# Group A's keys by residue of 16, strided attention on runs of 8 keys, and its queries copied by GpSimd

## The chip, the core and the metric

The program runs on one core of one Trainium2 chip. A core has TensorE (matmuls from SBUF into PSUM), VectorE, ScalarE, GpSimd, and SyncE, which issues the transfers; 16 DMA engines move data between HBM and SBUF. The engines run in parallel, each takes its own instructions in order, and they wait for each other through semaphores. The metric is the time of one execution on the device in microseconds.

## What is computed

One layer of a decoder with four groups of four heads (A to D), sequence 2048, head dimension 64. After a projection, each group attends in its own way, and the gated results go through an output projection. The change is in group A, which attends three times and merges: over 129 neighbours (rate 1), over every 4th token, and over every 16th.

```python
DILATED_CONFIGS = ((128, 1), (512, 4), (2048, 16))

def dilated_attention(q, k, v, table_h):
    b, nh, s, dh = q.shape
    outs, lses = [], []
    for window, rate in DILATED_CONFIGS:
        fold = lambda t: t.reshape(b, nh, s // rate, rate, dh).transpose(0, 3, 1, 2, 4).reshape(b * rate, nh, s // rate, dh)
        o, lse = banded_attention(fold(q), fold(k), fold(v), table_h, window // rate, dist_scale=rate)
...
    wts = jax.nn.softmax(jnp.stack(lses, axis=0), axis=0)
    return jnp.sum(wts[..., None] * jnp.stack(outs, axis=0), axis=0).astype(q.dtype)

def banded_attention(q, k, v, table_h, max_dist, dist_scale=1, sink=None):
    # query m attends keys m-j, 0 <= j <= max_dist, in blocks of 128 queries
...
    s = jnp.einsum('bhnqd,bhnkd->bhnqk', qb, kk).astype(jnp.float32) * (dh ** -0.5)
...
    s = s + rel_bias(dist * dist_scale, table_h).transpose(2, 0, 1)[:, None]
    p, m, den = masked_probs(s, valid, sink)
    o = jnp.einsum('bhnqk,bhnkd->bhnqd', p, vv.astype(jnp.float32)) / den

def reference(x, ...):
    h = rms_norm(x, norm_w[layer]) @ w_in[layer]
...
    o_a = dilated_attention(rms_norm(heads(a_q), g[0]), rms_norm(heads(a_k), g[1]), heads(a_v), tables[0])
...
    y = jnp.concatenate([merge(o_a), merge(o_b), merge(o_c), merge(o_d)], axis=-1) * jax.nn.silu(silu_gate)
    x = x + y @ w_out[layer]
```

## The kernel before

The kernel projects the groups in the order C, D, A, B, and attends in the order C, D, then A and B together. Projections and the output projection are written as generators of small steps, "fillers". A driver (`drive`) keeps a modelled clock for every engine (`T`), advanced by `op` with an expected duration for each instruction, and picks the next step for TensorE: attention steps whose inputs the model says are there, otherwise a filler step. The resulting order is fixed when the program is built; on the chip only semaphores decide when each instruction runs.

For queries and keys, `project` normalises a tile of 128 tokens and `turn` (L741) transposes it, four tiles at a time, from 128 tokens x 128 features into PSUM as features x tokens. `split` writes a high and a low half (two numbers that add up to the value) to HBM, `tqA` and `tkA`, tokens in order.

Strided attention of group A (`make_a`, `a_unit`) runs over 4 heads, rates 16 and 4, and 4 values of q0: 32 units. A unit has four blocks j of 128 queries. `qk_load` brings the whole head's queries (`wb` or `AQ`) and keys (`wb` or `keys`) into SBUF, tokens in order, for even and odd heads in turn; the next head's loads are issued in six pieces during units 1 to 6 of the current head. A score (L1639) is two matmuls per block: the block's 128 queries are the weights, 128 or 256 keys are the moving columns. Both are slices with a step of r words. At rate 16 a block has 128 keys; at rate 4 all blocks but the first of a residue have 256 (own and previous block): per head and rate 32 matmuls, at rate 4 24 of them with 256 columns.

Behind a half unit's scores VectorE adds the bias and takes the maximum (L1644, one reduction per block), scales the two maxima by -1 (L1649), ScalarE exponentiates (L1655), TensorE transposes the weights (L393), ScalarE and VectorE split them (L399, L403), TensorE multiplies with the values (L422), ScalarE copies the result (L371), TensorE transposes it back (L435) and VectorE adds its two halves (L439). After rate 4 of each head the two rates are merged, on GpSimd in the main (L1754, L1756), and stored.

Then 16 units of rate 1 of group A (`make_a1`) alternate with 16 units of group B (`make_b`, scores in L1941). The rate-1 units use the same `a_unit` with keys in contiguous slices, 60 of their 64 blocks with 256 keys.

The output projection (`out_proj`) is the filler of this part of the program: a tile's y and gate are loaded, gated (GpSimd L2102), transposed (L2112), and multiplied with the output weights (L2148) in 64 runs of 12 matmuls of 512 columns in all, first for groups C and D, then for A and B.

The planner's cost of a score and the two slices stand in these lines:

```python
e = op("PE", mm(n) if r == 1 else max(217.0, 0.92 * n)) + 60.0
...
c0 = rho + r * 128 * (i - i0)
return slice(c0, c0 + (n - 1) * r + 1, r)
```

Of the kernel before, what the change touches and what calls it, by code (L numbers as in the profile page):

```python
# [102 lines left out]
def tile_hybrid_heads(ctx, tc, a):  # L103
# [527 lines left out]
    def project(g, first=None):  # L631
# [104 lines left out]
        def turn(t3, j, gi, keep):  # L736
# [3 lines left out]
            for i in range(4):  # L740
                PE.transpose(ps[:, i * 128:(i + 1) * 128], keep[i][0][:, j * 128:(j + 1) * 128], ident)  # L741
# [827 lines left out]

    def qk_load(h, x):  # L1570

        q, k = QK[h % 2]
        n = S // 2
        if x < 2:
            aready[h] = load_q(q[:, x * n:(x + 1) * n].unsqueeze(1), "A", h, 1, x * n, n)
        else:
            c = slice((x - 2) // 2 * n, ((x - 2) // 2 + 1) * n)
            aready[h] = mv(raw(k)[x % 2::2, :, c], TK["A"][h * 64:h * 64 + 64, :, c])

# [29 lines left out]
    def group_ab():  # L1609
      with tc.tile_pool(name="aw", bufs=2) as aw, tc.tile_pool(name="as", bufs=1) as as_:  # L1610
# [8 lines left out]


        def a_unit(r, q0, setup, room, need, source, stats, close):
# [5 lines left out]
            def scores(half):  # L1627
# [7 lines left out]
                for j in (2 * half, 2 * half + 1):  # L1635
                    n = 128 * (1 + prevs[j])
                    s0 = (j % 2) * 256
                    for x in range(2):
                        PE.matmul(ps[:, s0:s0 + n], lhsT=qs(j), rhs=ks(x, j, prevs[j]), start=(x == 0), stop=(x == 1))  # L1639
                        e = op("PE", mm(n) if r == 1 else max(217.0, 0.92 * n)) + 60.0  # L1640
                for j in (2 * half, 2 * half + 1):
                    n = 128 * (1 + prevs[j])
                    s0 = (j % 2) * 256
                    V.tensor_tensor_reduce(P[:, j, :n], ps[:, s0:s0 + n], rev(H, n - 1, n), 1.0, LOW,  # L1644
                                           OP.add, OP.max, mx[:, j:j + 1])
                    e = op("DVE", vv(n), e)
# [11 lines left out]
                defer(e, weights)  # L1658

# [22 lines left out]
        def make_a(n):  # L1682
# [8 lines left out]

            def setup():
                if h < 3 and 1 <= n % 8 <= 6:
                    qk_load(h + 1, n % 8 - 1)
                if q0 == 0:
# [80 lines left out]
            def room():  # L1776
                if not have_all("A"):
# [3 lines left out]
            u = a_unit(r, q0, setup, room, lambda: max(at("s"), aready[h]), source,  # L1781
                       lambda: tiles(res[h, r][0]), close)
# [39 lines left out]
        def make_a1(m):  # L1822
            q0, h = AORDER[m]

            def source():
                Q, K, lo = As[m][0], As[m][1], As[m][7]
                return ((lambda j: Q[:, j * 128:(j + 1) * 128]),
                        (lambda x, j, p: K[:, x, (q0 + j - p - lo) * 128:(q0 + j + 1 - lo) * 128]), raw(A1H(h)))
# [12 lines left out]
            def setup():  # L1841
                if m == 0:
# [3 lines left out]
                    parts += [as_.tile([128, 1024], F32R, name="ow%d" % i) for i in range(2)]  # L1846
# [180 lines left out]
    def out_weights(half, places):  # L2027


        def load(i, after=0.0):  # L2030
            k, c = OCH[i]
            rw = px.tile([128, 512], F32, name="raw", bufs=4)
            r0 = ROW0[half] + k * 128
            e = mv(rw, a["w_out"][r0:r0 + 128, c * 512:(c + 1) * 512], after)
            if half == "CD" and i in olocked:
                oparked[i] = (e, lambda: split(i, rw, e))
            else:
                defer(e, lambda: split(i, rw, e))

        def split(i, rw, e):  # L2040
# [5 lines left out]
            def low():  # L2046
                V.scalar_tensor_tensor(l, rw, 0.5, h, op0=OP.mult, op1=OP.subtract)
                oready[half, OCH[i]] = op("DVE", vv(512) + 62.0, e)
                if i + OAHEAD < 8:
# [6 lines left out]
    def out_proj():  # L2056
# [19 lines left out]
        def load(n):  # L2076
# [3 lines left out]
            for i, g in enumerate(half):  # L2080
                mv(yt[:, i * 256:(i + 1) * 256], y_d[g][rows, :])
            gt = px.tile([128, 512], F32, name="raw", bufs=4)
            e = mv(gt, gate_d[rows, ROW0[half]:ROW0[half] + 512])
            defer(e, lambda: gate(n, yt, gt, e))
# [8 lines left out]
        def gate(n, yt, gt, e):  # L2093
# [5 lines left out]
            def rest():  # L2099
                V.scalar_tensor_tensor(th, th, 1.0, gt, op0=OP.add, op1=OP.mult)  # L2100
                e2 = op("DVE", vv(512), e)
                G.tensor_tensor(yt, yt, th, op=OP.mult)  # L2102
# [124 lines left out]
```

## Time and profile before

| | |
|---|---|
| time, median of 3 runs | 1796.22 us (1788.68 to 1797.0) |
| profiled execution | 1786.75 us, of which the span of instructions is 1785.0 |
[...]
| TensorE matmuls | busy 96% of the span |
| VectorE, ScalarE, GpSimd | busy 75%, 60%, 39% |
| HBM | 172 GB/s over the span |

Busy shares are means over stages that have different limits; the last 425 us, from 1360 us on, hold everything that the change touches but the key transposes. Matmuls overlap, so a matmul's duration isn't what the next one waits; the distance from one start to the next is. Line numbers are those of the kernel before.

### The profile page before, as it was taken

What the parts mean: (1) busy time and instruction counts of PE and PEld (TensorE: products, weight loads), DVE (VectorE), ACT (ScalarE), POOL (GpSimd) and SP (SyncE); (2) the same over time, 40 slices, a digit from 0 to 9 for tenths busy, and PEclk for the clock granted to TensorE, in tenths of its full rate; (3) what the DMA queues carried; (4) which work ended last, traced back from release to release, by engine and by line L of the source; (5) the groups of instructions that cost most, each with busy time, mean ns of one, the idle gap of its engine ahead of it and who ended that gap; (6) DMA issues with size and microseconds to landing.
All of it is one profiled execution on the core that took longest, in us unless ns stands there. A gap on an engine that the chain in (4) does not pass through costs nothing.

```text
span 1785.0 us, 31766 instructions
## 1 busy us (share of the span) xinstructions
PE 1715.9 (96%) x10035; PEld 1503.3 (84%) x10035; DVE 1332.7 (75%) x4072; ACT 1072.1 (60%) x2586; POOL 688.4 (39%) x841
## 2 busy tenths in 40 slices
PE   7989999999998999899989999999999999999999
PEld 5878878888787888688877889999879998888887
DVE  5446778998899996688567778887167777888883
ACT  4445556666676765567555667676256776576661
POOL 4666564544454554112353632222521111423231
PEclk9999999999999999999998999999999999999999
DMA  7763554344446324831485333323375768999986
GB/s 244 227 206 115 165 170 159 99 125 138 125 130 202 100 93 144 229 102 57 142 250 180 123 93 86 109 62 96 103 239 163 233 209 266 293 326 304 303 280 215
DMA packets 283480, 308.24 MB, mean 173 GB/s; under 512 B 80256, under 2 KB 201216, under 8 KB 282640
## 3 DMA queue, kind: packets, MB, share of 16 engines
q1 hardware_dynamic: 283312, 306.21, 55.7%
q8 instruction: 80, 1.31, 0.3%
q14 instruction: 88, 0.72, 0.1%
HBM read 219.47 MB, written 86.92 MB: 172 GB/s over the span
## 4 chain that ended last, share of the span: by engine, by line
PE 44%; DMA 4%; DVE 4%; issue 3%; POOL 2%; SPq 1%; ACT 1%; POOLq 0%; DVEq 0%; ACTq 0%
PE o L422 8%; PE j L833 8%; PE j L2148 7%; PE pt L393 7%; PE s L943 4%; PE s L1639 3%; PE pt L435 2%; PE s L1329 1%; DMA wb<-tkA 1%; SPq L156 1%; DMA DQ<-tqD 1%; PE s L1428 1%; PE pt L2112 1%; POOL xl L577 1%; PE s L1941 0%
## 5 line engine op out<-in xcount | busy, mean ns | idle before, releaser
L833 PE MATMUL j<-wb,xh 128*128 128x512 f32 (+2 forms) x2048 | 619.4, 383 | 12.6 <-ACT wb L618 8.0
L833 PEld LDWEIGHTS j<-wb,xh 128*128 128x128 f32 x2048 | 372.4, 191 | 58.6 <-issue 12.2
L833 PE MATMUL j<-wb,xl 128*128 128x512 f32 (+2 forms) x1024 | 386.1, 377 | 1.3 <-POOL xl L577 1.3
L403 DVE TENSOR_TENSOR pl<-pt,ph 128x512 fp32r<-128x512 f32 (+4 forms) x486 | 312.0, 659 | 40.6 <-ACT ph L399 40.2
L399 ACT ACTIVATE ph<-pt 128x512 fp32r<-128x512 f32 (+4 forms) x486 | 265.3, 575 | 123.5 <-PE pt L393 116.8
L833 PEld LDWEIGHTS j<-wb,xl 128*128 128x128 f32 x1024 | 194.7, 190 | 27.7 <-POOL xl L577 2.7
L679 POOL TENSOR_TENSOR ss<-ss,expo 128x6 f32<-128x6 f32 (+2 forms) x64 | 117.1, 1829 | 213.6 <-DVE ss L677 202.3
L577 POOL TENSOR_TENSOR xl<-xt,xh 128x512 fp32r<-128x512 f32 x112 | 150.1, 1340 | 9.3
L371 ACT ACTIVATE ot<-o 128x512 f32<-128x512 f32 (+1 forms) x160 | 81.5, 509 | 108.9 <-PE o L422 108.4
L943 PE MATMUL s<-keys,Q 128*128 128x512 f32 (+3 forms) x320 | 113.1, 400 | 10.9 <-DVE mx L945 5.5
L2102 POOL TENSOR_TENSOR xt<-xt,sq 128x512 f32<-128x512 f32 x32 | 41.3, 1289 | 197.9 <-DVE sq L2100 85.8
L571 POOL TENSOR_SCALAR xh<-xt 128x512 fp32r<-128x512 f32 x128 | 85.5, 668 | 76.4 <-DMA xt<-in_xt_dram 47.5
L660 ACT ACTIVATE stqk<-j 128x512 f32<-128x512 f32 x64 | 38.3, 598 | 122.5 <-PE j L833 122.3
L945 DVE CUSTOM_DVE_ANT_0 prow<-s,Hs 128x512 f32<-128x512 f32 (+3 forms) x160 | 94.6, 606 | 18.1 <-PE s L943 11.4
L674 DVE TENSOR_REDUCE ss<-sq 128x6 f32<-128x384 f32 (+2 forms) x64 | 39.4, 616 | 92.0 <-ACT sq L664 91.9
L1059 DVE SCALAR_TENSOR_TENSOR pa<-pb,ra,pa 128x1024 f32<-128x1024 f32 (+4 forms) x96 | 103.5, 1105 | 2.3
L945 DVE CUSTOM_DVE_ANT_0 pa<-s,H 128x512 f32<-128x512 f32 (+3 forms) x160 | 93.7, 604 | 14.4 <-PE s L943 12.6
L1655 ACT ACTIVATE ap<-ap,AO 128x128 f32<-128x128 f32 (+1 forms) x192 | 86.4, 454 | 18.6 <-DVE AO L1649 16.7
L945 DVE CUSTOM_DVE_ANT_0 pb<-s,H 128x512 f32<-128x512 f32 (+3 forms) x160 | 92.8, 604 | 4.3 <-PE s L943 3.5
L435 PE MATMUL pt<-ident,ot 128*128 128x128 f32 x512 | 85.4, 279 | 5.2 <-ACT ot L371 5.0
L1043 ACT ACTIVATE pa<-pa,nm 128x128 f32<-128x128 f32 (+7 forms) x64 | 76.9, 1201 | 21.6 <-DVE nm L951 21.1
L1523 ACT ACTIVATE prow<-prow,nm 128x128 f32<-128x128 f32 (+7 forms) x64 | 76.8, 1201 | 15.3 <-DVE nm L951 7.3
(266 smaller groups left out, 4201.7 us busy)
## 6 DMA issues: line engine op xcount, KB each, us to landing
xt<-in_xt_dram SPq DMA_DIRECT2D x128, 256.0 KB, 3.5
xr<-in_x_dram SPq DMA_DIRECT2D x16, 512.0 KB, 5.6
Q<-tqC SPq DMA_DIRECT2D x64, 128.0 KB, 3.4
DQ<-tqD SPq DMA_DIRECT2D x16, 512.0 KB, 4.5
raw<-gate_d SPq DMA_DIRECT2D x32, 256.0 KB, 4.3
stqk<-in_x_dram SPq DMA_DIRECT2D x32, 256.0 KB, 4.8
acc_d<-stqk SPq DMA_DIRECT2D x32, 256.0 KB, 4.5
stqk<-acc_d SPq DMA_DIRECT2D x32, 256.0 KB, 4.1
```

What stands on the lines that cost most here:

```text
L393: PE.transpose(ps[:rows, x * 128:(x + 1) * 128], src(), ident)
L399: A.activation(ph[:rows, :n], ps[:rows, :n], AF.Copy)
L403: V.tensor_tensor(pl[:rows, :n], ps[:rows, :n], ph[:rows, :n], op=OP.subtract)
L422: PE.matmul(u["po"][:, c0:c0 + wd], lhsT=lhsT(), rhs=x[:rows, col:col + wd], start=u["k"] == 1, stop=u["k"] == total, skip_group_check=True)
L435: PE.transpose(ps[:, i * 128:(i + 1) * 128], ot[:, i * 128:(i + 1) * 128], ident)
L577: G.tensor_tensor(l, xt, h, op=OP.subtract)
L679: G.tensor_tensor(ss[:, :nh], ss[:, :nh], expo[:, :nh], op=OP.pow)
L833: PE.matmul(ps[:, :n], lhsT=xx[:, ks], rhs=W[k][ww][:, lo:hi], start=(k == 0 and i == 0), stop=(k == KT - 1 and i == 2))
L943: PE.matmul(ps[:, :n], lhsT=q(), rhs=k[:, k0:k0 + n], start=(i == 0), stop=(i == np_ - 1))
L945: V.tensor_tensor_reduce(st["row"][:, k0:k0 + n], ps[:, :n], rev(H, t * 128 + 127 - k0, n), 1.0, LOW, OP.add, OP.max, st["mx"][:, ci:ci + 1])
L1059: V.scalar_tensor_tensor(rows[i][:, k0:k0 + n], part[i][:, k0:k0 + n], ra[:, 1:2], rows[i][:, k0:k0 + n], op0=OP.mult, op1=OP.add)
L2148: PE.matmul(ps, lhsT=xx[:, ks], rhs=OW[half, (k, c)][ww], start=(x == 0 and k == 0 and i == 0), stop=(x == len(halves) - 1 and k == 3 and ...
```

## The change

Keys of group A are stored in another order. Inside each tile of 128 tokens, token 16 i + r goes to place 8 r + i: all tokens of one residue of 16 lie side by side, in runs of 8. The reordering is done by the key transposes (`turn`, j >= 2), which write their PSUM columns with a step.

- Rate 16 reads 16 runs of 8 keys, one of each tile, in the right order.
- Rate 4 reads four runs of 8 from each tile (a residue of 4 holds four residues of 16); its score columns come out as (residue, run), and VectorE's reduction reads them from PSUM with a step to put them back in order.
- Rate 1 reads its one or two tiles residue by residue, in runs of 8, and its reduction reads with a step likewise.

The strided queries are no longer weights with a step: `gather_more` has GpSimd copy the four blocks of a unit side by side into one of four slots of 512 columns (two tiles `ow0`, `ow1`, which before were taken later for output weights). A slot is free when the unit that read it has its scores; the copies for the next head wait until its load is expected. The planner counts 1150 ns for a copy and, for a strided score, the same as for a contiguous one. Besides, the buffers `raw` of the output projection are now tracked by the planner, which holds back a load while none is free.

```diff
@@ turn
-                PE.transpose(ps[:, i * 128:(i + 1) * 128], keep[i][0][:, j * 128:(j + 1) * 128], ident)
+                to = ps[:, i * 128:(i + 1) * 128]
+                if g == "A" and j >= 2:
+                    to = to.rearrange("p (r i) -> p i r", r=16)
+                PE.transpose(to, keep[i][0][:, j * 128:(j + 1) * 128], ident)
@@ group_ab
+        OW4 = [as_.tile([128, 1024], F32R, name="ow%d" % i) for i in range(2)]
+        AC = {}
+
+        def gather_more():
+            while len(AC) < len(ORDER) and ORDER[len(AC)][0] in aloaded and free("AC", 4) < INF:
+                n = len(AC)
+                h, r, q0 = ORDER[n]
+                hd = alloc("AC", 4)
+                C = OW4[hd[1] % 4 // 2][:, hd[1] % 2 * 512:hd[1] % 2 * 512 + 512]
+                Q = QK[h % 2][0].rearrange("p (c r) -> p r c", r=r)
+                if r == 16:
+                    G.tensor_copy(C.rearrange("p (j c) -> p j c", j=4), Q[:, q0:q0 + 4])
+                else:
+                    G.tensor_copy(C, Q[:, q0 // 4])
+                AC[n] = (C, hd, op("POOL", 1150.0, max(aready[h], hd[2])))
@@ a_unit, scores
-                        e = op("PE", mm(n) if r == 1 else max(217.0, 0.92 * n)) + 60.0
+                        e = op("PE", mm(n)) + 60.0
...
-                    V.tensor_tensor_reduce(P[:, j, :n], ps[:, s0:s0 + n], rev(H, n - 1, n), 1.0, LOW,
+
+                    fr = ps[:, s0:s0 + n] if r == 16 else ps[:, s0:s0 + n].rearrange("p (b u) -> p u b", b=16 // r)
+                    V.tensor_tensor_reduce(P[:, j, :n], fr, rev(H, n - 1, n), 1.0, LOW,
@@ make_a
+            def scored():
+                release(AC[n][1], T["PE"] + 60.0)
+                defer(T["PE"] + 100.0, gather_more)
...
-                Q, K = QK[h % 2]
-
-                def cols(j, i0, n):
-                    rho, i = divmod(q0 + j, nb)
-                    c0 = rho + r * 128 * (i - i0)
-                    return slice(c0, c0 + (n - 1) * r + 1, r)
-                return (lambda j: Q[:, cols(j, 0, 128)]), (lambda x, j, p: K[:, x, cols(j, p, 128 * (1 + p))]), Hs[h, r]
+                K, C = QK[h % 2][1], AC[n][0]
+                if r == 16:
+                    K = K.rearrange("p x (t r c) -> p x r t c", t=16, r=16)
+                    ks = lambda x, j, p: K[:, x, q0 + j]
+                else:
+                    K = K.rearrange("p x (t s a c) -> p x a s t c", s=4, a=4, c=8)[:, :, q0 // 4]
+                    ks = lambda x, j, p: K[:, x, :, (j - p) * 4:(j + 1) * 4]
+                return (lambda j: C[:, j * 128:(j + 1) * 128]), ks, Hs[h, r]
@@ make_a1, source
-                        (lambda x, j, p: K[:, x, (q0 + j - p - lo) * 128:(q0 + j + 1 - lo) * 128]), raw(A1H(h)))
+                        (lambda x, j, p: K[:, x].rearrange("p (t b c) -> p b t c", b=16, c=8)[:, :, q0 + j - p - lo:q0 + j + 1 - lo]),
+                        raw(A1H(h)))
@@ out_proj, prepare
-            while n < min(len(PARTS), at_["part"] + 3) and (n < 2 or n - 2 in zready) and there(*PARTS[n]):
+            while n < min(len(PARTS), at_["part"] + 3) and (n < 2 or n - 2 in zready) and there(*PARTS[n]) and free("raw", 4) < INF:
```

The new costs also move instructions. On TensorE, at the first units of strided attention (head 0, rate 16), `s` is a score, `j` the output projection, `pt` a transpose of gated rows (`xt`) or of attention weights (`ap`). Before:

```order
L1639 MATMUL s<-wb 128x128 x12
L2148 MATMUL j<-wb,xh 128x512 x2
L2148 MATMUL j<-wb,xl 128x512
L1639 MATMUL s<-wb 128x128 x4
L2112 MATMUL pt<-ident,xt 128x128 x4
L393 MATMUL pt<-ident,ap 128x128 x4
L1639 MATMUL s<-wb 128x128 x12
L393 MATMUL pt<-ident,ap 128x128 x4
```

Of the change:

```order
L1663 MATMUL s<-wb,ow_17186 128x128 x8
L2190 MATMUL j<-wb,xh 128x512 x2
L2190 MATMUL j<-wb,xl 128x512
L1663 MATMUL s<-wb,ow_17186 128x128 x8
L2190 MATMUL j<-wb,xh 128x512 x2
L2190 MATMUL j<-wb,xl 128x512
L393 MATMUL pt<-ident,ap 128x128 x4
L1663 MATMUL s<-wb,ow_17187 128x128 x8
L2190 MATMUL j<-wb,xh 128x512 x2
L2190 MATMUL j<-wb,xl 128x512
L2154 MATMUL pt<-ident,xt 128x128 x4
```

Where one step of the output projection stood among the first 28 scores, three stand now. Counted over the whole order, 75 matmuls of the output projection stood between the first strided score and the first rate-1 score, and 153 do now; between the first score of the first rate-1 unit and that of the last 420 and now 393; behind that 231 and now 177.

On GpSimd, around the merge of head 0 (`AO`), with copies of queries (`ow`) and gating (`xt`) beside it. Before:

```order
L2102 TENSOR_TENSOR xt<-xt,sq 128x512 x3
L1754 TENSOR_TENSOR AO<-AO,mg 128x16x65 x2
L1756 TENSOR_TENSOR AO<-AO 128x16x65
L1757 COPY AO<-mgn 128x16
```

Of the change:

```order
L1638 COPY ow_17186<-AQ 128x512 x2
L1638 COPY ow_17187<-AQ 128x512 x2
L1640 COPY ow_17186<-AQ 128x512
L2144 TENSOR_TENSOR xt<-xt,sq 128x512
L1640 COPY ow_17186<-AQ 128x512
L1640 COPY ow_17187<-AQ 128x512 x2
L1791 TENSOR_TENSOR AO<-AO,mg 128x16x65 x2
L1793 TENSOR_TENSOR AO<-AO 128x16x65
L1794 COPY AO<-mgn 128x16
```

The eight copies of head 1 stand ahead of the first merge, one gating among them; the copies stand in the same queue as gating and merges.

## Rows read from the trace of the kernel before

**Rows 1.** The page, part 1 (busy time, share, instructions) and part 4 (chain).

```profile
PE 1715.9 (96%) x10035; PEld 1503.3 (84%) x10035; DVE 1332.7 (75%) x4072; ACT 1072.1 (60%) x2586; POOL 688.4 (39%) x841
...
PE 44%; DMA 4%; DVE 4%; issue 3%; POOL 2%; SPq 1%; ACT 1%; POOLq 0%; DVEq 0%; ACTq 0%
```

**Rows 2.** Busy us of each engine in three stretches, granted clock, DMA share, GB/s.

```profile
1363.00:1500.00 137.00, 135.87 (x848) 129.88 (x846) 100.94 (x407) 98.34 (x342) 24.35 (x16) 1.00 0.76 241
1501.00:1727.00 226.00, 220.18 (x1452) 194.96 (x1450) 193.78 (x659) 152.68 (x459) 71.52 (x97) 1.00 0.95 295
1735.00:1785.00 50.00, 46.22 (x213) 37.46 (x211) 20.32 (x32) 6.56 (x12) 9.78 (x10) 0.99 0.69 222
```

**Rows 3.** Groups by line and shape, 1360 to 1500: busy us, mean ns, idle before.

```profile
L1639 PEld LDWEIGHTS s<-keys,AQ 128*128 128x128 f32 x128 | 30.8, 318 | 0.4 <-DVE amx L1644 0.3
...
L422 PEld LDWEIGHTS o<-ph,tl 128*128 128x128 f32 x59 | 11.4, 193 | 0.0
```

**Rows 4.** TensorE's timeline, strided scores of head 0: start, length, instruction, count.

```profile
1367.85 2.83 PE L1639 MATMUL s<-wb 128*128 128x128 f32 x12
1370.49 0.62 PE L393 MATMUL pt<-ident,ap 128*128 128x128 f32 x4
1370.87 1.09 PE L1639 MATMUL s<-wb 128*128 128x128 f32 x4
...
1380.12 2.23 PE L1639 MATMUL s<-wb 128*128 128x256 f32 x8
1382.16 0.24 PE L422 MATMUL o<-ph,th 128*128 128x128 f32 x1
```

**Rows 5.** TensorE's timeline, contiguous operands: products of head 0, rate-1 scores.

```profile
1372.10 0.27 PE L422 MATMUL o<-pl,tl 128*128 128x128 f32 x1
1372.21 0.27 PE L422 MATMUL o<-ph,tl 128*128 128x128 f32 x1
...
1609.20 1.20 PE L1639 MATMUL s<-wb 128*128 128x256 f32 x8
1610.24 0.63 PE L2148 MATMUL j<-wb,xh 128*128 128x512 f32 x2
```

**Rows 6.** VectorE's groups by line and shape, whole span: reductions, scaling, PSUM reads.

```profile
L403 DVE TENSOR_TENSOR pl<-pt,ph 128x512 fp32r<-128x512 f32 x388 | 259.4, 684 | 33.0 <-ACT ph L399 32.7
L1649 DVE TENSOR_SCALAR AO<-amx 128x2 f32<-128x2 f32 x96 | 24.6, 256 | 3.6
L1644 DVE CUSTOM_DVE_ANT_0 ap<-s,wb 128x256 f32<-128x256 f32 x60 | 23.1, 419 | 3.9 <-PE s L1639 3.9
L1644 DVE CUSTOM_DVE_ANT_0 ap<-s,AH 128x256 f32<-128x256 f32 x48 | 18.9, 419 | 4.4 <-PE s L1639 4.4
L439 DVE TENSOR_REDUCE AO<-pt 128x256 f32<-128x512 f32 x27 | 18.6, 689 | 18.0 <-PE pt L435 18.0
L775 DVE TENSOR_TENSOR sq<-pt,post 128x512 f32<-128x512 f32 x8 | 8.8, 1104 | 0.7 <-PE pt L741 0.7
```

**Rows 7.** GpSimd's groups by line and shape, whole span: 512-word operations.

```profile
L577 POOL TENSOR_TENSOR xl<-xt,xh 128x512 fp32r<-128x512 f32 x112 | 150.1, 1340 | 9.3
L571 POOL TENSOR_SCALAR xh<-xt 128x512 fp32r<-128x512 f32 x128 | 85.5, 668 | 76.4 <-DMA xt<-in_xt_dram 47.5 <-PE j L833 16.6 <-PE o L422 5.7
```

**Rows 8.** All engines' timeline around a merge on GpSimd at 1443.9.

```profile
1443.21 0.42 DVE L1644 CUSTOM_DVE_ANT_0 ap<-s,AH 128x256 f32<-128x256 f32 x1 [0.54 <-PE s L1639]
...
1443.91 3.82 POOL L1754 TENSOR_TENSOR AO<-AO,mg 128x1040 f32<-128x1040 f32 x2 [29.39 <-ACT mg L1751]
1444.02 1.85 DVE L1649 TENSOR_SCALAR AO<-amx 128x2 f32<-128x2 f32 x1
```

**Rows 9.** TensorE's timeline in the tail: output projection alone.

```profile
1735.48 0.62 PE L2148 MATMUL j<-keys,xh 128*128 128x512 f32 x2
1735.94 0.40 PE L2148 MATMUL j<-keys,xl 128*128 128x512 f32 x1
1736.17 0.62 PE L2148 MATMUL j<-keys,xh 128*128 128x512 f32 x2
```

More of the change, by code (lines that the diff above doesn't have):

```diff
@@ L1568, in tile_hybrid_heads @@
     aready = {}
+    aloaded = set()
     def qk_load(h, x):
@@ L1578, in qk_load @@
             aready[h] = mv(raw(k)[x % 2::2, :, c], TK["A"][h * 64:h * 64 + 64, :, c])
+        if x == 5:
+            aloaded.add(h)
     ORDER = [(h, r, q0) for h in range(4) for r in (16, 4) for q0 in range(0, 16, 4)]
@@ L1617, in h_load, with a_unit @@
             Hs[h, r] = H
-        def a_unit(r, q0, setup, room, need, source, stats, close):
+        OW4 = [as_.tile([128, 1024], F32R, name="ow%d" % i) for i in range(2)]
[12 more added lines that the diff above has]
+                AC[n] = (C, hd, op("POOL", 1150.0, max(aready[h], hd[2])))
+        def a_unit(r, q0, setup, room, need, source, stats, close, scored=lambda: None):
             nb = 16 // r
@@ L1658, in scores @@
                 defer(e, weights)
+                if half:
+                    scored()
             jobs = []
@@ L1690, in tiles @@
                 return O[:, q0:q0 + 4] if nb == 1 else O[:, q0 // nb::r]
+            def scored():
+                release(AC[n][1], T["PE"] + 60.0)
+                defer(T["PE"] + 100.0, gather_more)
             def setup():
+                if n == 0:
+                    gather_more()
                 if h < 3 and 1 <= n % 8 <= 6:
                     qk_load(h + 1, n % 8 - 1)
+                    if n % 8 == 6:
+                        defer(aready[h + 1], gather_more)
                 if q0 == 0:
@@ L1779, in room @@
                 return 0.0 if q0 else free("AO", 4)
-            u = a_unit(r, q0, setup, room, lambda: max(at("s"), aready[h]), source,
-                       lambda: tiles(res[h, r][0]), close)
+            u = a_unit(r, q0, setup, room, lambda: max(at("s"), aready[h], AC[n][2] if n in AC else INF), source,
+                       lambda: tiles(res[h, r][0]), close, scored)
             u["after"] = after
@@ L1845, in setup @@
                     parts += [QK[1][0][:, i * 1024:(i + 1) * 1024] for i in range(2)]
-                    parts += [as_.tile([128, 1024], F32R, name="ow%d" % i) for i in range(2)]
+                    parts += OW4
                     out_weights("AB", [(w[:, 0:512], w[:, 512:1024]) for w in parts])
@@ L2031, in load, with split @@
             k, c = OCH[i]
+            hd = alloc("raw", 4)
             rw = px.tile([128, 512], F32, name="raw", bufs=4)
             r0 = ROW0[half] + k * 128
-            e = mv(rw, a["w_out"][r0:r0 + 128, c * 512:(c + 1) * 512], after)
+            e = mv(rw, a["w_out"][r0:r0 + 128, c * 512:(c + 1) * 512], max(after, hd[2]))
             if half == "CD" and i in olocked:
-                oparked[i] = (e, lambda: split(i, rw, e))
+                oparked[i] = (e, lambda: split(i, rw, e, hd))
             else:
-                defer(e, lambda: split(i, rw, e))
-        def split(i, rw, e):
+                defer(e, lambda: split(i, rw, e, hd))
+        def split(i, rw, e, hd):
             h, l = places[i]
@@ L2048, in low @@
                 oready[half, OCH[i]] = op("DVE", vv(512) + 62.0, e)
+                release(hd, oready[half, OCH[i]])
                 if i + OAHEAD < 8:
@@ L2081, in load @@
                 mv(yt[:, i * 256:(i + 1) * 256], y_d[g][rows, :])
+            hg = alloc("raw", 4)
             gt = px.tile([128, 512], F32, name="raw", bufs=4)
-            e = mv(gt, gate_d[rows, ROW0[half]:ROW0[half] + 512])
-            defer(e, lambda: gate(n, yt, gt, e))
+            e = mv(gt, gate_d[rows, ROW0[half]:ROW0[half] + 512], hg[2])
+            defer(e, lambda: gate(n, yt, gt, e, hg))
         def r_load(n):
@@ L2091, in r_load, with gate @@
                 mv(R[n, c][0], src[t * 128:(t + 1) * 128, c * 512:(c + 1) * 512])
-        def gate(n, yt, gt, e):
+        def gate(n, yt, gt, e, hg):
             hd = alloc("sq", 1)
@@ L2101, in rest @@
                 e2 = op("DVE", vv(512), e)
+                release(hg, e2)
                 G.tensor_tensor(yt, yt, th, op=OP.mult)
```

## The prediction

> **What bounds the kernel now.** I read the totals first: TensorE is busy 96% of the 1785.0 us span and half of the chain that ended last runs over it [rows 1]. Then I cut the end of the program into three stretches [rows 2]: strided attention (1363 to 1500 us), the window-128 attention of groups A and B (1501 to 1727), and the rest of the output projection (1735 to the end). In the first TensorE lacks 1.1 of 137 us, in the second 5.8 of 226. VectorE, ScalarE and the DMA engines stand at about three quarters in the first stretch; in the second the DMA share is 0.95. So TensorE's own work sets the end, and the output projection, a filler that the driver puts wherever the attention steps are not ready, keeps it so. A saving on TensorE is worth its full size only as long as this filler can still cover every wait.
>
> The place of the change is the strided scores. Their weight loads take 318 ns where a weight load from a contiguous tile beside them takes 193 [rows 3]. The durations of matmuls overlap, so I take start to next start: 12 matmuls of 128 columns at rate 16 take 1367.85 to 1370.49, 0.220 us each; 8 at rate 4 take 1380.12 to 1382.16, 0.255 us each [rows 4]. With contiguous operands a 128-column matmul follows its neighbour after 0.110 us, and 8 window-128 scores take 1609.20 to 1610.24, 0.130 us each [rows 5]. Reading every 16th or every 4th word costs about double, on either operand.
>
> **The change, part by part.**
>
> 1. *Scores.* 4 heads x 4 units x 8 = 128 matmuls at rate 16 and 128 at rate 4. Now 128 x 0.220 + 128 x 0.255 = 60.8 us. If copied queries and keys in runs of 8 words are read at the contiguous pace, 128 x 0.110 + 128 x 0.130 = 30.7 us. Saved: 30.1 us. No row shows a moving operand in runs, so the bounds are the contiguous pace (30.1) and the strided pace (rival B). I take the contiguous end: the price now is about the same at steps of 4 and of 16 words, which looks like a cost per separate word, and a run of 8 has one break where the old pattern had eight.
>
> 2. *Window-128 scores* of A now also read runs of 8. By the same choice 0; at the other end 120 of their 128 matmuls (256 columns) go from 0.130 to 0.255, +15.0 us (in rival B).
>
> 3. *Key transposes.* 2 blocks x 4 x 4 = 32 transposes write PSUM at a step of 8 words. Contiguous ones take 0.095 us (four from 1370.49 to 1370.87) [rows 4]. No row shows a strided write by TensorE; doubling it, as the strided read doubles, is 32 x 0.095 = 3.0 us, the other end is 0. I take the middle, 1.5 us, since neither row is nearer. [...]
>
> 4. *VectorE reads the scores back in order*, with a step in PSUM: 64 reductions at rate 4 and 64 in the window part, 419 ns for 256 columns now. The reduction of the output transposes also alternates between words 64 apart in PSUM and takes 689 ns for 512, as the plain subtraction does (684): cost 0. The other end is the addition that writes SBUF with a step, 1104 ns: (1104 - 684) / 512 = 0.82 ns per word [rows 6]. I take 0, because the first row reads PSUM with a step as the new operand does; the second is rival A.
>
> 5. *GpSimd copies.* 32 copies of 128x512. Nearest rows: one-input 668 ns, two-input 1340 ns [rows 7]. GpSimd is busy 24 of 137 us here [rows 2], and four slots let a copy run four units ahead, so its length is hidden as such; only the first score waits for a copy, 0.7 to 1.3 us in which filler stands ready. What isn't hidden: a GpSimd operation holds up one kind of VectorE operation. At 1443.91 a merge starts on GpSimd; the two-column scaling of the maxima behind it starts at 1444.02 and takes 1.85 us, until GpSimd's first merge is done; its usual time is near 0.17, its mean 256 ns [rows 8, 6]. ScalarE's exponentials, and then the transposes, are queued behind that scaling. A copy starts when TensorE has read its slot, just when VectorE starts on the same unit's last two reductions; the scaling comes 0.81 us behind them (1443.21 to 1444.02). So a copy of c us holds VectorE c - 0.81 us: 0 for 0.67, 0.53 for 1.34, which is 0 to 17 us over 32 copies. The excess of this scaling over 170 ns is 96 x 86 ns = 8.3 us now, and TensorE lost at most 1.1 us to it in the strided stretch; at that ratio 17 us cost 2.3. [...]
>
> 6. *Bookkeeping of the raw buffers* in the output projection adds no instruction; it lets the planner see a wait that the loads had anyway: 0, and if it did delay a load, three parts loaded ahead cover it.
>
> 7. *What the saved time exposes.* The order of instructions shows filler moving forward: the driver finds the scores done sooner and puts output projection between units. Before the first window-128 score stand 78 more of these matmuls, between there and the last such unit 27 fewer, behind it 54 fewer. One takes 0.69 / 3 = 0.23 us (1735.48 to 1736.17) [rows 9]. So the strided stretch shrinks only to 137 - 30.1 + 78 x 0.23 + 1.3 (transposes of their inputs) = 126 us, the middle one by 6, the tail by 12. In the tail 213 TensorE operations come with 20.3 us of VectorE and 0.69 x 50 = 34.5 us of DMA [rows 2]; for 91 that is 8.7 and 14.7. VectorE in the strided stretch: 100.9 + 8.7 + holds of 0 to 17 = 110 to 127 of 126 us; DMA 104 + 14.7 = 119 of 126. Both fit, closely. For holds and waits in this denser stretch I take off 3.5 us: 2.3 from item 5 and some for the DMA engines, which at 0.95 in the middle stretch go with 2.6% of TensorE idle against 0.8% in the first.
>
> Sum: -30.1 + 1.5 + 3.5 = -25.1 us. The profiled span becomes 1760 us and that execution 1762 instead of 1786.75; the median of the runs shown, 1796.22, lies 9.5 us above the profiled one, so I forecast 1771.
>
> **Rivals.**
>
> A. *The stepped PSUM reads cost 0.82 ns a word.* Rate 4: 48 x 256 + 16 x 128 = 14,336 words, 11.8 us; window part 60 x 256 + 4 x 128 = 15,872, 13.0 us. VectorE then needs 122 to 139 of 126 us in the strided stretch, and 207 of 220 behind it. About half of the 24.8 us reaches TensorE: 1783. For it the stepped write row, against it the stepped PSUM read row.
>
> B. *Runs of 8 are read no faster than single words.* The weights are contiguous now, so rate 16 still comes down: 128 columns at the strided pace of 0.255 / 256 = 1.0 ns a column are 0.128 us, a saving of 11.8. Rate 4 stays, the window part loses 15.0, the transposes and waits 5: 8 us worse, or, if part of the 0.255 is the strided weights and the columns run at 0.85 ns (0.218 for 256), 3 better. About no change: 1796. Against it that the step's size didn't matter. [...] The trace agrees that steps of 16 and 64 bytes are both slow; no run yet shows a run of 8.
>
> C. *Slower: the copies hold VectorE longer than filler can cover.* Place: the scaling behind each unit's reductions. VectorE has 110 us besides; to eat the whole gain it must need 126 + 28.6 = 155 us, which is a hold of 1.4 us per unit and a copy of 2.2 us. At 2.5 us the stretch is 164 us and the time 1806. No GpSimd row of 512 words is above 1.34 us; a copy with a step is not in the trace.
>
> D. *DMA engines become the bound* in the strided stretch, at 119 of 126 us: values or the next head's keys land late, and TensorE waits in order. If they need a tenth more, 5 us are lost there and as much behind it: 1781. For it the 0.95 of the middle stretch, against it that TensorE idles only 2.6% there.
>
> **Numbers.** Forecast 0.64, A 0.13, D 0.09, B 0.09, C 0.05. The forecast's own range is 1763 to 1779 (transposes 0 to 3.0, waits 0 to 9). Out to most of A and D on one side and to none of the losses on the other, 1760 to 1788 holds about 0.84. A measurement of this kernel can tell about 0.5%, 9 us: faster means under 1787. Forecast, most of A and D are faster: 0.82. B and the ends of A, D and C are the same: 0.13. Slower: 0.05.
>
> **What would show it.** Right: strided weight loads near 190 ns; 0.11 and 0.13 us between scores; reductions still at 419 ns with the stepped operand; copies under 1.3 us; the stretch from first strided to first window-128 score near 126 us; the tail behind the last attention unit some 12 us shorter. Wrong: 256-column scores at 0.2 us or more (B), reductions near 630 ns (A), a mean of the scaling far over 0.8 us with idle TensorE before transposes (C), TensorE released by loads of queries, keys or values (D).

## The result and the profile after

The changed kernel takes 1867.36 us (median of 4 runs, 1865.67 to 1868.16) against 1795.62 us for the kernel before beside it: a ratio of 1.0411, 95% interval [1.039, 1.0431]. It is 4% slower; the forecast was 1771 us. The profiled execution has a span of 1864.8 us, 80 us over the span before; the medians are 72 us apart, since the execution profiled before was one of the shorter ones.

The page of the changed kernel, parts 1 and 4, stands against [rows 1]:

```profile
PE 1720.7 (92%) x10035; PEld 1501.7 (81%) x10035; DVE 1335.4 (72%) x4072; ACT 1069.6 (57%) x2587; POOL 721.5 (39%) x873
...
PE 41%; DMA 6%; DVE 4%; issue 4%; POOL 3%; SPq 1%; ACT 1%; POOLq 0%; DVEq 0%; ACTq 0%
```

TensorE's busy time is not lower but 5 us higher, its share of the span and of the chain is down, and DMA's share of the chain is up from 4% to 6%. The three stretches of [rows 2], cut at the first strided score (1369), the first window-128 score of group A (1512) and shortly behind the last one (1807; that one starts at 1804); columns as there:

```profile
1369.00:1512.00 143.00, 132.53 (x940) 121.18 (x941) 113.63 (x426) 101.46 (x354) 62.03 (x51) 0.95 0.86 275
1512.00:1807.00 295.00, 230.11 (x1381) 203.52 (x1380) 187.22 (x630) 145.44 (x437) 67.40 (x91) 0.87 0.70 214
1807.00:1865.00 58.00, 50.57 (x246) 41.18 (x244) 25.06 (x59) 13.80 (x35) 12.96 (x16) 0.93 0.51 168
```

The loss is in the middle one: 295 us instead of 226, with 65 us of idle TensorE instead of 5.8, a granted clock of 0.87 instead of 1.00 (1.00 is full speed), and a DMA share down from 0.95 to 0.70. So it isn't for want of DMA bandwidth. What TensorE waited for from 1340 us to the end (engine, line, releaser: us, times, longest):

```profile
PE s L1663 <- DMA wb<-tkA: 44.9, 8, 11.6
PE s L1663 <- issue: 10.4, 1, 10.4
PE pt L2154 <- POOL xt L2144: 8.6, 3, 4.6
PE pt L435 <- DVE pl L403: 4.1, 1, 4.1
```

Line 1663 is the score matmul, `wb<-tkA` the load of the keys of a window-128 unit. In the trace before, no wait of this kind is among TensorE's waits from 1340 us on; the largest there is

```profile
PE pt L435 <- ACT ot L371: 3.9, 2, 2.8
```

The transfer itself is as fast as before (at the median 5.6 us from issue to landing for loads of 320 KB, against 6.1), so the question is which transfer a score waits for. First SyncE's queue, on the timeline of the changed kernel (start, length, instruction, count):

```profile
1567.29 1.17 SPq L156 DMA_DIRECT2D wb<-tkA  x2
1574.03 1.17 SPq L156 DMA_DIRECT2D wb<-tkA  x2
1590.39 1.17 SPq L156 DMA_DIRECT2D wb<-tkA  x2
```

And TensorE's scores between these loads, on the same timeline:

```profile
1578.66 0.33 PE L1663 MATMUL s<-wb 128*128 128x128 f32 x2
1580.80 0.97 PE L1663 MATMUL s<-wb 128*128 128x256 f32 x6 [1.81 <-DMA wb<-tkA]
1581.61 0.63 PE L2190 MATMUL j<-wb,xh 128*128 128x512 f32 x2
...
1589.62 0.74 PE L1663 MATMUL s<-wb 128*128 128x256 f32 x4
...
1595.43 1.19 PE L1663 MATMUL s<-wb 128*128 128x256 f32 x4 [4.14 <-DMA wb<-tkA]
```

A unit has 8 score matmuls and two loads of keys, and units alternate between two slots of the tile `wb`. The unit that starts at 1578.66 uses the loads issued at 1567.29. Its first two scores (one block of 128 keys) run; the third stands until 1580.80, some 6 us behind the loads issued at 1574.03, which are the next unit's and go to the other slot. The next unit does the same: it starts at 1589.62, stops in its middle, and goes on at 1595.43, when the loads of the unit behind it (1590.39) are in. Where a unit stops like this, loading one unit ahead is undone: it ends only when the next one's keys have landed. Nine of the 16 units do. The wait put down to "issue" is one of them: it ends at 1702.34, when the loads of keys issued at 1694.83 are in.

The clock falls with it. The same stretch in pieces of 5 us (TensorE's busy time, granted clock, DMA share, GB/s):

```profile
1590.00:1595.00 5.00, 1.29 (x11) 0.86 0.67 184
1595.00:1600.00 5.00, 4.57 (x18) 0.50 0.62 192
...
1610.00:1615.00 5.00, 0.76 (x7) 0.90 0.60 182
1615.00:1620.00 5.00, 0.00 (x0) 0.50 0.85 246
1620.00:1625.00 5.00, 2.65 (x10) 0.50 0.71 219
```

Behind these two waits TensorE works at a granted clock of 0.50 for about 5 us, half of full speed, and the work behind such a wait takes longer too: four scores take 1.19 us from 1595.43 on, against 0.74 before the wait.

Meanwhile the scores, reductions and copies came out close to the prices that the prediction gave them. First TensorE's timeline of strided scores, at rate 16 and at rate 4, against [rows 4, 5]:

```profile
1403.34 1.01 PE L1663 MATMUL s<-keys,ow 128*128 128x128 f32 x8
1404.18 0.68 PE L2190 MATMUL j<-wb,xh 128*128 128x512 f32 x2
...
1416.86 1.25 PE L1663 MATMUL s<-keys,ow 128*128 128x256 f32 x8
1417.95 0.64 PE L2190 MATMUL j<-wb,xh 128*128 128x512 f32 x2
```

From start to next start, 8 of them take 0.84 us at rate 16 and 1.09 us at rate 4: 0.105 and 0.136 us each, instead of 0.220 and 0.255. The window-128 scores, which now read runs of 8 too, are 0.135 us apart (six from 1580.80 to 1581.61), against 0.130. Their weight loads as groups from 1350 us on (busy, mean ns, idle), against [rows 3]:

```profile
L1663 PEld LDWEIGHTS s<-wb,ow 128*128 128x128 f32 x128 | 18.1, 207 | 2.8 <-POOL ow L1638 2.3 <-issue 0.3
L1663 PEld LDWEIGHTS s<-keys,ow 128*128 128x128 f32 x128 | 17.0, 194 | 3.3 <-issue 2.8 <-DVE amx L1670 0.3
```

They are down from 318 to about 200 ns. VectorE's scaling and reductions, against [rows 6]:

```profile
L1675 DVE TENSOR_SCALAR AO<-amx 128x2 f32<-128x2 f32 x96 | 30.6, 318 | 3.6
L1670 DVE CUSTOM_DVE_ANT_0 ap<-s,wb 128x256 f32<-128x256 f32 x60 | 23.1, 419 | 60.4 <-PE s L1663 60.1
L1670 DVE CUSTOM_DVE_ANT_0 ap<-s,AH 128x256 f32<-128x256 f32 x48 | 18.8, 416 | 0.6 <-PE s L1663 0.6
```

GpSimd's copies, against the neighbours of [rows 7]:

```profile
L1638 POOL CAST ow<-wb 128x512 fp32r<-128x512 f32 x8 | 8.2, 1067 | 2.0 <-DMA yD<-Os 2.0
L1640 POOL CAST ow<-wb 128x512 fp32r<-128x512 f32 x8 | 8.9, 1124 | 10.3 <-PE s L1663 10.3
```

### The profile page after: what moved, and what is told of

Its sections match the earlier page's. It is cut to its first block, busy times and chain, and to the rows that moved or that the text cites. A ratio compares the mean times of both kernels' runs of the same rounds, so it can differ in the third digit from the quotient of the medians.

```text
span 1864.8 us, 31863 instructions
## 1 busy us (share of the span) xinstructions
PE 1720.7 (92%) x10035; PEld 1501.7 (81%) x10035; DVE 1335.4 (72%) x4072; ACT 1069.6 (57%) x2587; POOL 721.5 (39%) x873
## 4 chain that ended last, share of the span: by engine, by line
PE 41%; DMA 6%; DVE 4%; issue 4%; POOL 3%; SPq 1%; ACT 1%; POOLq 0%; DVEq 0%; ACTq 0%
PE j L836 8%; PE o L422 8%; PE pt L393 7%; PE j L2190 6%; PE s L946 4%; DMA wb<-tkA 2%; PE s L1663 2%; PE pt L435 2%; PE s L1332 1%; SPq L156 1%; PE s L1431 1%; PE s L1979 1%; DMA wb<-vvA 1%; PE pt L2154 1%; POOL xl L577 1%
## 5 line engine op out<-in xcount | busy, mean ns | idle before, releaser
L2190 PE MATMUL j<-wb,xh 128*128 128x512 f32 x256 | 86.2, 419 | 0.0
```

The lines of the kernel that those rows point to most:

```text
L2190: PE.matmul(ps, lhsT=xx[:, ks], rhs=OW[half, (k, c)][ww], start=(x == 0 and k == 0 and i == 0), stop=(x == len(halves) - 1 and k == 3 and ...
```

## The experiments

Three theories stood at first: (1) the bookkeeping of the raw buffers delays loads; (2) the planner's new, lower cost of a strided score makes a worse order; (3) the layout, the copies and the stepped accesses themselves bring the waits. Four kernels take these apart.

**Without the bookkeeping** (the changed kernel, the old text of the loads):

```diff
-            hd = alloc("raw", 4)
...
-            e = mv(rw, a["w_out"][...], max(after, hd[2]))
+            e = mv(rw, a["w_out"][...], after)
```

> The change without the planner's tracking of the raw buffers, all else kept. Theory 1 (the tracking holds back and reorders the output projection's loads, so that the rate-1 key loads stand late in SyncE's queue): about 1770 us, and TensorE's waits for keys of the rate-1 units fall from 45 us to under 10. Theory 2 (the new cost of a strided score makes the plan run ahead of the chip): stays at 1850 to 1870. Theory 3 (layout and copies themselves, whatever the plan): stays at 1850 to 1870.

Measured: 1841.18 us, ratio to before 1.026 [1.024, 1.028]. 26 us come back, 46 stay.

**The bookkeeping alone** on the kernel before (the same lines, added):

> The kernel before with the planner's tracking of the raw buffers alone; scores, keys and queries as before. Theory 1: slower than before by 40 us or more (1835 and up). Theories 2 and 3: as before, 1790 to 1800.

Measured: 1798.56 us, 1.0016 [1.0005, 1.0027]. It costs next to nothing by itself, so theory 1 falls as the main cause. Why it costs 26 us in the changed kernel isn't shown by these two runs.

**The old cost of a strided score** in the changed kernel:

```diff
-                        e = op("PE", mm(n)) + 60.0
+                        e = op("PE", mm(n) if r == 1 else max(217.0, 0.92 * n)) + 60.0
```

> The change with the planner's old cost of a strided score (217 to 235 ns), so that filler stays nearly where it stood before (105 output-projection matmuls ahead of the first rate-1 score as against 117 before and 198 with the change). Theory 2: 1765 to 1785 us, because the 30 us of faster scores become slack and not earlier filler. Theory 1 or 3: 1840 or more.

Measured: 1854.62 us, 1.0343 [1.0318, 1.0368]. 13 us come back.

**Both undone:**

> Layout, copies and stepped reads of the change, with the old score cost and without the tracking: the plan is nearly that of before. Theories 1 and 2: 1760 to 1785. Theory 3 (layout and copies slow the stretch by themselves): over 1830.

Measured: 1856.8 us, 1.0341 [1.0322, 1.0359], with 9 waits of TensorE for `wb<-tkA` in the window-128 stretch, 43.5 us in all. Theory 2 falls as the main cause, and theory 3 is left. Since the waits are all at window-128 scores, the suspect was the one thing that the change does there: the view through which they read their keys. (A view is the form in which the program names part of a tile, with its lengths and steps.) I split theory 3 into F, the view makes a false wait, one that the data doesn't ask for, for the other slot's load, and G, the layout and copies cost by themselves.

**Plain keys for the window-128 scores:**

```diff
-    (lambda x, j, p: K[:, x].rearrange("p (t b c) -> p b t c", b=16, c=8)[:, :, q0 + j - p - lo:q0 + j + 1 - lo]),
+    (lambda x, j, p: K[:, x, (q0 + j - p - lo) * 128:(q0 + j + 1 - lo) * 128]),
```

> The changed kernel, but the window-128 scores of group A read the keys of a tile as they lie, as 256 contiguous words, instead of in runs of 8 through the view that splits the words of the whole slot in three levels. The reductions still undo the order, so the key order of group A's window-128 scores is not restored in this run: it stands for time alone. Theory F (false wait): in the changed kernel the score of one unit waits for the key loads of the next unit in the other half of the same tile, since the split view is taken to touch the whole tile; in the order of instructions with its waits a first-of-unit score waits for 3 loads before the change and for up to 4 more behind it. F expects: TensorE idle behind 1340 us under 20 us (after: 79), unit spacing back near 13.3 us, granted clock of the run 0.98 or more, 1768 to 1785 us. Theory G (the plan, the copies and the reordered loads themselves leave TensorE waiting, whatever the view): 1840 us or more. Runs of 8 being slow to read would give at most 15 us back, 1850.

Measured: 1801.46 us, 1.0052 [1.003, 1.0074]. 66 of the 72 us are gone, far more than slow reads could explain (15). But the time isn't the 1768 to 1785 of the expectation either.

**The view alone** on the kernel before (the same edit the other way round):

> The kernel before with one edit: the window-128 scores of group A read their keys through the split view in runs of 8, nothing else changed (keys still lie in order, so the columns of these scores come out in another order: it stands for time alone). Theory F expects the false wait here too: TensorE released by loads of the next unit's keys, 30 us or more of idle time in the window-128 stretch, granted clock falling under 0.97, 1825 to 1860 us. Theory G and slow reads: 1796, or at most 15 us more if runs of 8 are read slowly (1811).

Measured: 1854.31 us, 1.034 [1.0298, 1.0382]: 59 us for one view. TensorE's waits at scores from 1340 us on, none of which the kernel before has:

```profile
PE s L1639 <- DMA wb<-tkA: 21.5, 5, 4.7
PE s L1639 <- issue: 15.0, 3, 5.5
PE s L1639 <- DMA raw<-gate_d: 8.5, 1, 8.5
```

Its window-128 stretch (TensorE's busy time, granted clock, DMA share, GB/s):

```profile
1501.00:1790.00 289.00, 237.96 (x1464) 0.93 0.78 236
```

TensorE is idle for 51 us of it, against 5.8 of 226.

The order of instructions shows what the edit adds. One unit on TensorE in the kernel before (in brackets the semaphores that an instruction waits for):

```
6870 L1639 MATMUL s<-wb 128x128 [waits DMAHW4_49,DMAHW3_49,DMAHW2_49]
6871 L1639 MATMUL s<-wb 128x128
6872 L1639 MATMUL s<-wb 128x256 x6
```

The same unit with the view:

```
6871 L1639 MATMUL s<-wb 128x128 [waits DMAHW4_49,DMAHW3_49,DMAHW2_49]
6872 L1639 MATMUL s<-wb 128x128
6873 L1639 MATMUL s<-wb 128x256 [waits DMAHW5_49,DMAHW4_49]
6874 L1639 MATMUL s<-wb 128x256 x5
```

The first score waits for its own three loads in both; the first score with 256 columns waits for two more queues. The two transfers that these semaphores count up to are the next unit's two loads of keys, into the other slot. Nothing in the data asks for that, since the slots don't overlap: the framework that builds the program inserts it, from the view. What in its bookkeeping does so isn't shown.

**Reorder in PSUM instead**: keys read plainly, the destination in runs of 8. This computes what the reference does.

```diff
-    PE.matmul(ps[:, s0:s0 + n], lhsT=qs(j), ...)
+    to = ps[:, s0:s0 + n]
+    if r == 1:
+        to = to.rearrange("p (b t c) -> p t b c", b=16, c=8)
+    PE.matmul(to, lhsT=qs(j), ...)
```

> The changed kernel, with the reorder moved from the moving operand to the destination: the window-128 scores of group A read 256 contiguous key words, and write them to PSUM in runs of 8 at the place that the split view gave them. What is computed is the reference's. Theory F expects the time of the run with plain keys if a stepped PSUM write costs nothing (key transposes with such a write took 270 ns at the median, as the others do): 1768 to 1785 us. If the stepped write costs as much as a strided read, 120 matmuls take 0.13 us more: 15 us, 1783 to 1800. Theory G: 1840 or more.

Measured: 1802.05 us, 1.0044 [1.0028, 1.0061], the same as with plain keys (1801.46). So a matmul that writes PSUM in runs costs nothing that shows, and the false wait is worth 1867.4 - 1802.1 = 65 us. Its three stretches (columns as in [rows 2]):

```profile
1367.00:1507.00 140.00, 129.34 (x940) 118.48 (x941) 113.30 (x426) 101.44 (x354) 62.14 (x51) 0.98 0.88 277
1507.00:1740.00 233.00, 219.14 (x1384) 192.72 (x1384) 186.69 (x630) 145.72 (x438) 67.81 (x91) 0.95 0.88 273
1740.00:1797.00 57.00, 49.76 (x244) 40.30 (x242) 24.79 (x59) 13.55 (x35) 12.74 (x16) 0.96 0.54 175
```

Its waits from 1367 us on:

```profile
PE pt L2157 <- POOL xt L2147: 7.4, 2, 4.7
PE pt L435 <- DVE pl L403: 4.1, 1, 4.1
PE s L1666 <- DVE amx L1673: 2.6, 1, 2.6
PE pt L435 <- DVE xl L2167: 2.5, 1, 2.5
...
PE s L1666 <- POOL ow L1638: 1.9, 1, 1.9
```

TensorE is idle for 10.7 us in the strided stretch (before 1.1) and for 13.9 in the middle one (5.8), and the clock lost in the three is 0.02 x 140 + 0.05 x 233 + 0.04 x 57 = 17 us. The 30 us saved in the scores go there. The longest wait, 4.7 us at 1506, is at the output projection itself, for the gating of its inputs. It and the 2.6 us for VectorE, which end at 1493, come from loads of the output projection: VectorE and GpSimd stand for a tile of x and for a gate, while the DMA engines are nearly full (first two rows: start, length, instruction, what it waited for; then columns as in [rows 2]):

```profile
1491.94 0.69 DVE L2199 TENSOR_TENSOR stqk<-j,stqk 128x512 f32<-128x512 f32 x1 [5.45 <-DMA stqk<-in_x_dram]
1504.67 1.26 POOL L2147 TENSOR_TENSOR xt<-xt,sq 128x512 f32<-128x512 f32 x1 [16.82 <-DMA raw<-gate_d]
1484.00:1506.00 22.00, 14.72 (x91) 12.65 (x89) 12.44 (x50) 10.62 (x38) 2.54 (x2) 0.99 0.97 309
```

So 7.3 of the 10.7 us of the strided stretch go back to loads.

**And without the bookkeeping:**

> The same as the run with the reorder in PSUM, and the bookkeeping of the raw buffers in the output projection taken out again. Alone on the kernel before it cost 1.0016 [1.0005, 1.0027]; taken out of the changed kernel it gave 26 us back, which by theory F was only a different meeting of false waits. F expects within 8 us of the run with the reorder in PSUM; if the bookkeeping is itself a cost, 15 us or more below it.

Measured: 1793.26 us, 0.9991 [0.9975, 1.0006], 9 us less. That lies between the two expectations and tells them apart poorly: the bookkeeping costs something here, though next to nothing on the kernel before. Of the 26 us that it cost with the false wait in, 9 are left without it.

**The old cost with the reorder in PSUM** (the edit of the third run). Theory H: the filler that the lower cost moves forward is itself late; K: the waits come whatever the plan.

> The run with the reorder in PSUM, with the planner's old cost of a strided score (217 ns or 0.92 ns a column), so that fewer matmuls of the output projection are put between the strided units. With the false wait gone, 30 us of TensorE work are saved, yet the time is 1802: the trace shows 27 us of idle TensorE behind 1340 us (before: about 8), in single waits of 2 to 5 us for the gating of the projection's inputs and for VectorE held by GpSimd, and a granted clock of 0.83 to 0.97 in the stretches that hold them. Theory H (the filler that was moved forward is itself late, and its waits with the clock behind them eat the saving): with less of it moved, idle time under 15 us, 1775 to 1790 us. Theory K (the waits come from the copies and from engines that are simply full, whatever the plan): within 6 us of 1802.

Measured: 1785.13 us, 0.9946 [0.993, 0.9962]. 17 us come back by moving less filler, as H has it. Strided and middle stretch:

```profile
1366.00:1492.00 126.00, 116.10 (x829) 104.80 (x830) 103.10 (x403) 94.64 (x333) 57.08 (x47) 0.95 0.77 240
1492.00:1713.00 221.00, 215.38 (x1412) 190.44 (x1410) 187.13 (x645) 151.07 (x458) 70.51 (x92) 0.99 0.98 304
```

The middle stretch is whole again (5.6 us idle, clock 0.99). The strided one isn't: 9.9 us idle and a clock of 0.95. But its waits are other ones: the longest is now the 1.9 us for the first copy, and none goes back to a load.

The false wait can be priced in five pairs of runs that differ in the reorder alone: 65 us in the whole change, 59 on the kernel before, 48 without the bookkeeping, 69 with the old cost, 71 with both undone.

**Both undone, reorder in PSUM:**

> The reorder in PSUM, with both the old cost and without the bookkeeping of the raw buffers: the layout, the copies and the stepped accesses alone, under a plan as near to that of before as can be had. Theory H: 1770 to 1785 us, the least of all these runs. Theory K: as the run without the bookkeeping, 1788 to 1798.

Measured: 1785.78 us, 0.995 [0.9933, 0.9967], no better than with the bookkeeping. The old plan sets the 17 us, not the bookkeeping.

**Without the copies** (queries read with their step, reorder in PSUM, new cost):

```diff
...
-    G.tensor_copy(C, Q[:, q0 // 4])
...
-    return (lambda j: C[:, j * 128:(j + 1) * 128]), ks, Hs[h, r]
...
+    qs = lambda j: Q[:, q0 + j:q0 + j + 127 * 16 + 1:16]
...
+    qs = lambda j: Q[:, q0 // 4 + 512 * j:q0 // 4 + 512 * j + 127 * 4 + 1:4]
+    return qs, ks, Hs[h, r]
```

> The run with the reorder in PSUM, without GpSimd's copies: the queries are read as weights with the step of 16 or 4 words, as before, the keys in runs of 8. It tells what the copies are worth and what they cost. If the strided weights set the old pace by themselves, strided scores stay 0.22 us apart, 25 to 30 us of TensorE time come back, and the time is 1815 to 1832. If the keys' step set it, scores are at 0.11 to 0.14 us and the time is 1802 less what the copies cost: by theory K (copies hold VectorE, the first score waits for one) 1785 to 1797, else 1802.

Measured: 1820.12 us, 1.0137 [1.0108, 1.0166]. TensorE's timeline at rate 16:

```profile
1374.06 1.94 PE L1660 MATMUL s<-wb 128*128 128x128 f32 x8
1375.84 0.68 PE L2192 MATMUL j<-wb,xh 128*128 128x512 f32 x2
```

And its weight loads as a group:

```profile
L1660 PEld LDWEIGHTS s<-keys,AQ 128*128 128x128 f32 x128 | 30.8, 318 | 1.2 <-issue 1.1
```

1.78 us for 8 are 0.223 each: with strided weights the scores stay at the old pace, though the keys are read in runs. The copies are worth 18 us, no strided score gets faster without them, and the part of theory K by which they cost more than they bring falls. The other half, copied queries with the keys still in order, was not run, so what the reordered keys bring by themselves isn't shown.

**The first unit without a copy**, with the old cost, since the first score waits 1.9 us for GpSimd, whose first copy waits for the last store of group D's result:

> The run with the reorder in PSUM and the old cost, in which the first strided unit reads its queries as they lie, with the step of 16 words, so that it doesn't wait for the first copy; the other 31 units take theirs from copies. In that run the first score waits 1.9 us for GpSimd, whose first copy waits for the last store of the attention before it; the granted clock of 1365 to 1400 us is 0.90 and of 1400 to 1450 0.93. Theory L (this wait costs itself and the clock behind it): the wait gone, the clock of 1365 to 1400 at 0.98 or more, less one strided unit of scores at the old pace (1 us): 1778 to 1782 us, 3 to 7 below 1785. Theory M (the short waits for VectorE after it, 0.3 to 1.3 us each, make the clock fall by themselves): the clock stays near 0.93 in that stretch and the time within 2 us of 1785.

Measured in five rounds: 1785.25 us, 0.9954 [0.9936, 0.9972], no different from 1785.13. The wait only moved to the second unit (1.4 us at 1368.46, ended by VectorE's scaling). The stretches around it and behind it, with the first copy (the run with the old cost; busy, granted clock, DMA share, GB/s):

```profile
1364.00:1370.00 6.00, 3.75 (x20) 0.85 0.56 161
1370.00:1375.00 5.00, 5.00 (x25) 0.50 0.82 316
```

And without it:

```profile
1364.00:1370.00 6.00, 4.57 (x24) 0.96 0.60 182
1370.00:1375.00 5.00, 4.92 (x31) 0.71 0.75 256
```

The clock rows side with L (a shorter wait, less time at 0.50), the time with M. Over the strided stretch the clock is 0.99 (1363 to 1490) instead of 0.95, some 5 us, but the idle time is 11.1 us instead of 9.9 and the stretch no shorter (127 us against 126). So a better clock alone gave nothing back that shows, and what of the time these waits and their clock cost stays open.

## Why the prediction was wrong

**The step that failed is item 2**, the window-128 scores. It asked what reading runs of 8 costs and put it at 0, and that price was right (0.135 us between scores against 0.130, 0.6 us for 120 of them). But it took the view for nothing except a way of reading. The view also decides what the score waits for, and the order of instructions, which was there to be read with its waits, shows the new one. 65 us hang on it. None of the rivals had it: B came nearest in place and was wrong in kind, C had the right direction from another mechanism, and D's sign, TensorE released by loads of keys, did show, but with the DMA share down at 0.70.

**Item 7, the filler, is the second.** It let 78 more matmuls of the output projection fill the strided stretch, gave 3.5 us for holds and waits, and put the stretch at 126 us. It measured 140 us with the false wait removed. Filler covers a wait only when its own inputs are there, and moved forward it needs its loads, its gating and its splitting sooner: VectorE goes to 113 of 140 us, the DMA share from 0.76 to 0.88. Both were computed as fitting, with means; the waits are single late arrivals, two of them, 7.3 us, for loads of the output projection. Moving less of it gave 17 us back, and those two waits went. Most of the idle time that went is in the middle stretch (13.9 to 5.6 us), though, where moving filler forward also leaves less of it; whether late inputs or missing filler cost more there wasn't taken apart. The prediction also had no term for the clock, because the rows before show 0.99 to 1.00 [rows 2]; with the false wait removed, the lower clock comes to 17 us of work at full speed.

The account: 1771 as forecast, + 65 (false wait, runs with and without it), + 17 (filler moved too far, runs with either cost), leaves 14 us. For these there are, in the strided stretch of the run with the old cost, the 9.9 us of idle time against 1.1 (the forecast allowed 3.5) and the 5% of clock (6 us). The idle time is in the main waits for VectorE (7 us) and for the first copy (1.9); the last run had the clock back without a gain in time, so how the 14 us divide is open. The sum holds along this chain of runs only: with the false wait still in, the old cost gave 13 us and not 17.

**What was right.** Item 1: 0.105 and 0.136 us between scores against 0.11 and 0.13, so that some 30 us are there. Rival B falls with it: the window-128 scores, too, read runs of 8 words at the contiguous pace (0.135 us against 0.130). That a step costs about double on either operand is shown for the weights alone (0.223 us a score with strided weights and keys in runs, 0.105 with copied ones); a step on the keys alone was not run. Item 3: the transposes that write PSUM at a step of 8 words stay at 280 ns in the mean of their group of 240, as before, so the middle value of 1.5 us was too much and the end at 0 the right one. The scores written in runs of 8 show no cost either (1802.05 us against 1801.46 with plain writes). Item 4: 416 and 419 ns with the stepped operand, so rival A falls. Item 5: copies of 1.07 to 1.12 us, inside the bounds; the scaling rises from 256 to 318 ns in the mean, 6 us over 96 of them, far from rival C's price. The hold isn't kept to the scaling, though: in the run with the reorder in PSUM, while GpSimd's last merge runs (from 1539.85 for 4.26 us), another operation of VectorE takes 2.28 us instead of 0.69, and the longest wait of the middle stretch, 4.1 us for VectorE, ends behind it at 1545. Item 6: 1.0016 by itself, but 9 us in the run with the reorder in PSUM, so the 0 holds for the kernel before and for the old cost only. The tail came out 7 us shorter, not 12: 60.8 us from the last window-128 score of A to the end, against 67.7. The terms of the forecast's own range, 0 to 3.0 and 0 to 9 us, add up to 1766 to 1778 and not 1763 to 1779; nothing hangs on it.

**Rival D** was right in part. With the false wait removed the DMA engines stand at 0.88 over the strided stretch, but at 0.97 in its last 22 us, and there 7.3 us of idle TensorE go back to loads that land late. They are the output projection's, x and gate, and not queries, keys or values.

## What to carry to other kernels

A view is part of the synchronization (59 us for one view on the kernel before): when an edit changes the pattern of an access to a tile that holds several buffers, compare the waits of the instructions before and after, not only their order, and put such a reorder on the side where it brings no wait for another slot (here on the PSUM side: 1802.05 us against 1801.46 with plain writes). Filler is cover only while its own inputs are there (7.3 us of idle TensorE here for loads that came late); if an edit makes the work around it shorter, check what feeds the filler, and try the old plan with the new kernel. The best version measured here is the change with the reorder in PSUM and the old cost, 1785.13 us, 0.9946 [0.993, 0.9962] of the kernel before.

## What the runs showed of the hardware

- In the run with the reorder in PSUM and the old cost, a wait of 1.9 us on TensorE was followed by a stretch of 5 us at a granted clock of 0.50 (1370 to 1375). In the kernel before, a wait of 2.8 us at 1535.7 wasn't: its stretch stands at 1.00 (TensorE's busy time, granted clock, DMA share, GB/s), so the length of the one wait doesn't decide alone.

```profile
1520.00:1550.00 30.00, 27.17 (x166) 1.00 0.93 287
```

- Steps in PSUM were free in each form tried: transposes of which 32 in 240 write at a step of 8 words (280 ns in the mean of the group, as before), scores written in runs of 8 (1802.05 us against 1801.46 with plain writes), and reductions that read 256 words at a step of 16 or 64 (419 and 416 ns).
- With weights read at a step, contiguous runs on the moving side bring nothing: 0.223 us a score at rate 16 against 0.220 before.
